# Rotary embedding on one core: 2 MB slabs in place of 1 MB tiles, small pieces at both ends, tables ordered anew

## The chip, the cores and the metric

The kernel runs on one core of one Trainium2 chip. The metric is the device time of one execution in microseconds, the median of ten runs. The engines that matter are VectorE (DVE in the profile), GpSimd (POOL), ScalarE (ACT), SyncE (SP), and the core's 16 DMA engines, which carry everything between HBM and the on-chip memory. SP and ScalarE each own a queue of transfers.

## The reference

`x` is float32 of shape (8, 2048, 8, 64): batch, position, head, channel. `cos` and `sin` are (2048, 32). The last axis of `x` is cut into halves and rotated by the position's angles:

```python
x1 = x[..., :32]; x2 = x[..., 32:]
cos = cos[None, :, None, :]; sin = sin[None, :, None, :]
out1 = x1 * cos - x2 * sin
out2 = x1 * sin + x2 * cos
return np.concatenate([out1, out2], axis=-1)
```

33.55 MB are read, 33.55 MB written, and the two tables are 256 KB each.

## The kernel before

The 2048 positions of a batch lie on the 128 partitions, 16 consecutive ones each (`R = 16`), so a partition's data of one batch are contiguous: 16 positions x 512 floats, 32 KB. A tile takes 4 positions (`SL = 4`) of one batch: 128 x 2048 floats, 1 MB, in rows of 8 KB. There are 32 tiles, and the loop takes all batches for the first four positions, then the next four. Twenty buffers (`xpool`) hold tiles.

The tables are loaded whole at the start by the ScalarE queue (lines 48 and 49), sin first; each is 128 x 512 floats in rows of 2 KB. VectorE makes from sin a table `ssin` with -sin and +sin for the two halves (lines 58 and 59) and copies cos into PSUM (`cos_ps`, line 60). The loads of all tiles stand in the sync queue (line 55).

A tile passes through three steps:
- POOL multiplies in two instructions of 128 x 1024 (line 73) the swapped halves of `xt` by `ssin` and writes `t2` in SBUF (three buffers).
- VectorE multiplies `xt` by cos (line 78) into `t1`, which lies in PSUM (one buffer).
- VectorE adds `t1` and `t2` into `xt` itself (line 83), and the ScalarE queue stores the tile (line 84).

The order of work is that of the program; the waits are set by a framework that follows which tile is read and written. A buffer of `xpool` is loaded again when the store from it has landed.

Of the kernel before, what the change touches and what calls it, by code (L numbers as in the profile page):

```python
# [2 lines left out]

# [4 lines left out]


@with_exitstack  # L10
def kernel(
    ctx: ExitStack,
    tc: tile.TileContext,
    x: bass.AP,
    cos: bass.AP,
    sin: bass.AP,
    out: bass.AP,
):
    nc = tc.nc
    f32 = mybir.dt.float32  # L20

    B, S, H, D = x.shape
    Dh = D // 2
    P = 128
    HD = H * D
    R = S // P

    SL = 4
    n_blk = R // SL
    FREE = SL * HD  # L30

    xv = x.rearrange("b (q r) h d -> b q (r h d)", q=P)
    ov = out.rearrange("b (q r) h d -> b q (r h d)", q=P)
    cos_src = cos.rearrange("(q r) d -> q r d", q=P)
    sin_src = sin.rearrange("(q r) d -> q r d", q=P)

    const_pool = ctx.enter_context(tc.tile_pool(name="const", bufs=1))
    cps_pool = ctx.enter_context(tc.tile_pool(name="cps", bufs=1, space=bass.MemoryType.PSUM))
    t1_pool = ctx.enter_context(tc.tile_pool(name="t1p", bufs=1, space=bass.MemoryType.PSUM))
    xpool = ctx.enter_context(tc.tile_pool(name="xpool", bufs=20))  # L40
    t2_pool = ctx.enter_context(tc.tile_pool(name="t2p", bufs=3))

    cos_sb = const_pool.tile([P, R, Dh], f32, tag="cb")
    sin_sb = const_pool.tile([P, R, Dh], f32, tag="sb")
    ssin = const_pool.tile([P, R, 2, Dh], f32, tag="ss")
    cos_ps = cps_pool.tile([P, R, Dh], f32, tag="cp")

    nc.scalar.dma_start(out=sin_sb, in_=sin_src)  # L48
    nc.scalar.dma_start(out=cos_sb, in_=cos_src)

    tiles = [(b, l) for l in range(n_blk) for b in range(B)]
    xts = []
    for i, (b, l) in enumerate(tiles):
        xt = xpool.tile([P, FREE], f32, tag="xt", name=f"xt{i}")
        nc.sync.dma_start(out=xt, in_=xv[b, :, l * FREE : (l + 1) * FREE])
        xts.append(xt)

    nc.vector.tensor_scalar_mul(ssin[:, :, 0, :], sin_sb, -1.0)  # L58
    nc.vector.tensor_copy(ssin[:, :, 1, :], sin_sb)  # L59
    nc.vector.tensor_copy(cos_ps, cos_sb)  # L60

    def rep(a, n):
        return dataclasses.replace(a, ap=[a.ap[0][:], a.ap[1][:], [0, n], a.ap[-1][:]])

    for i, (b, l) in enumerate(tiles):
        xt = xts[i]
        t1 = t1_pool.tile([P, FREE], f32, tag="t1")
        t2 = t2_pool.tile([P, FREE], f32, tag="t2")

        for u in range(2):  # L70
            dst = t2.rearrange("p (rh u d) -> p rh u d", u=2, d=Dh)[:, :, u, :]
            src = xt.rearrange("p (rh u d) -> p rh u d", u=2, d=Dh)[:, :, 1 - u, :]
            nc.gpsimd.tensor_mul(  # L73
                out=dst.rearrange("p (r h) d -> p r h d", h=H),
                in0=src.rearrange("p (r h) d -> p r h d", h=H),
                in1=rep(ssin[:, l * SL : (l + 1) * SL, u, :], H),
            )
        nc.vector.tensor_mul(  # L78
            out=t1.rearrange("p (r k d) -> p r k d", r=SL, d=Dh),
            in0=xt.rearrange("p (r k d) -> p r k d", r=SL, d=Dh),  # L80
            in1=rep(cos_ps[:, l * SL : (l + 1) * SL, :], 2 * H),
        )
        nc.vector.tensor_add(out=xt, in0=t1, in1=t2)  # L83
        nc.scalar.dma_start(out=ov[b, :, l * FREE : (l + 1) * FREE], in_=xt)


# [1 line left out]
_INS = ['x', 'cos', 'sin']  # L88
_OUTS = [((8, 2048, 8, 64), 'float32')]


# [23 lines left out]
```

## Time and profile before

| | us |
|---|---|
| median of 10 runs (168.19 to 168.55) | 168.3 |
| the profiled execution | 168.36 |
| its span on the core | 166.6 |
| VectorE busy, 67 instructions | 148.2 (89%) |
| GpSimd busy, 68 instructions | 146.3 (88%) |
| moved by DMA | 67.65 MB, mean 406 GB/s |

The span is what the profiler saw of the program on the core; the execution's own time is 1.76 us more. A busy figure counts instructions that compute, not those that issue transfers. The profile also has a chain of waits, which follows from the last instruction back to what released each step, groups of equal instructions with their mean duration and the idle time ahead of them, busy time and DMA rate for chosen stretches, and for each transfer the time from its issue to its landing.

### The profile page before, as it was taken

The numbers are of one execution on the slowest core, as the hardware profiler recorded it, in microseconds if no ns is written. First come the engines' busy times: TensorE is split into PE (matmuls) and PEld (weight loads), VectorE is DVE, ScalarE is ACT, GpSimd is POOL, SyncE is SP. The second block draws the span as 40 slices with busy tenths as digits, with TensorE's granted clock in tenths as the row PEclk, the third lists the DMA queues.
The fourth block names the chain that finished last, engine by engine and source line by source line (L and its number), as shares of the span: only waits on it lengthen the run. The fifth ranks groups of instructions, "written<-read, shape, count | busy, mean of one in ns | idle before, by whom it ended". The sixth has DMA issues, their size and how long they took to land.

```text
span 166.6 us, 381 instructions
## 1 busy us (share of the span) xinstructions
DVE 148.2 (89%) x67; POOL 146.3 (88%) x68
## 2 busy tenths in 40 slices
DVE  0169999999999999999999999999999999999980
POOL 0299999999999999999999999999999999998000
DMA  5999999999999999999999999999999999999656
GB/s 180 425 424 427 368 433 419 433 425 429 429 421 435 421 433 427 425 433 421 427 425 429 427 425 431 421 433 423 431 431 421 433 421 431 427 427 431 275 220 252
DMA packets 9506, 67.65 MB, mean 406 GB/s; under 512 B 1056, under 2 KB 1056, under 8 KB 1312
## 3 DMA queue, kind: packets, MB, share of 16 engines
q10 hardware_dynamic: 4896, 34.08, 48.6%
q1 hardware_dynamic: 4608, 33.56, 48.4%
q14 instruction: 2, 0.02, 0.0%
HBM read 34.08 MB, written 33.55 MB: 406 GB/s over the span
## 4 chain that ended last, share of the span: by engine, by line
DVE 89%; DMA 5%; issue 2%; DVEq 0%; ACTq 0%
DVE t L78 44%; DVE xt L83 44%; DMA cos_sb<-in_cos_dram 5%; DVE cos_ps L60 0%; DVEq L83 0%; ACTq L48 0%
## 5 line engine op out<-in xcount | busy, mean ns | idle before, releaser
L73 POOL TENSOR_TENSOR t<-xt,ssin 128x1024 f32<-128x1024 f32 x64 | 146.1, 2318 | 6.8 <-DVE ssin L58 6.8
L83 DVE TENSOR_TENSOR xt<-t,t 128x2048 f32<-128x2048 f32 x32 | 73.3, 2292 | 3.3
L78 DVE TENSOR_TENSOR t<-xt,cos_ps 128x2048 f32<-128x2048 f32 x32 | 73.5, 2295 | 1.1
L58 DVE TENSOR_SCALAR ssin<-sin_sb 128x512 f32<-128x512 f32 x1 | 0.4, 427 | 6.8 <-DMA sin_sb<-in_sin_dram 6.8
L60 DVE COPY cos_ps<-cos_sb 128x512 f32<-128x512 f32 x1 | 0.7, 695 | 2.4 <-DMA cos_sb<-in_cos_dram 2.4
L59 DVE COPY ssin<-sin_sb 128x512 f32<-128x512 f32 x1 | 0.4, 420 | 0.0
L99 POOL MEMSET const-float32-0.0<- 128x1 f32 x1 | 0.1, 98 | 0.2 <-issue 0.2
L99 POOL MEMSET const-bfloat16-1.0<- 128x1 bf16 x1 | 0.1, 101 | 0.0
L99 POOL MEMSET const-uint8-127<- 128x1 uint8 x1 | 0.1, 101 | 0.0
L99 POOL MEMSET const-float32-1.0<- 128x1 f32 x1 | 0.1, 98 | 0.0
## 6 DMA issues: line engine op xcount, KB each, us to landing
xt<-in_x_dram SPq DMA_DIRECT2D x32, 1024.0 KB, 20.8
out_dram<-xt ACTq DMA_DIRECT2D x32, 1024.0 KB, 11.3
sin_sb<-in_sin_dram ACTq DMA_DIRECT2D x1, 256.0 KB, 6.0
cos_sb<-in_cos_dram ACTq DMA_DIRECT2D x1, 256.0 KB, 8.7
```

Of the source, the lines that this page charges most:

```text
L58: nc.vector.tensor_scalar_mul(ssin[:, :, 0, :], sin_sb, -1.0)
L59: nc.vector.tensor_copy(ssin[:, :, 1, :], sin_sb)
L60: nc.vector.tensor_copy(cos_ps, cos_sb)
L73: nc.gpsimd.tensor_mul(out=dst.rearrange("p (r h) d -> p r h d", h=H), in0=src.rearrange("p (r h) d -> p r h d", h=H), in1=rep(ssin[:, l * ...
L78: nc.vector.tensor_mul(out=t1.rearrange("p (r k d) -> p r k d", r=SL, d=Dh), in0=xt.rearrange("p (r k d) -> p r k d", r=SL, d=Dh), in1=rep ...
L83: nc.vector.tensor_add(out=xt, in0=t1, in1=t2)
L99: nc = _bacc.Bacc("TRN2", target_bir_lowering=False, num_devices=1)
```

## The change

Transfers become 2 MB slabs of 8 positions (`SL = 8`, rows of 16 KB), in 10 buffers. VectorE and GpSimd still work on units of 4 positions, 128 x 2048 floats (`UNIT`), except in the first and the last slab. Slab 0 is loaded and worked on in pieces of 1, 1, 2 and 4 positions (512, 512, 1024 and 2048 floats a partition); the last slab is loaded whole, and worked on and stored in pieces of 4, 2, 1 and 1. All other slabs are stored whole, after their second unit.

The order of the tables is new: x's first piece of 256 KB leads the sync queue, then sin on the same queue, then the rest of x; cos leads the ScalarE queue. `ssin` is gone: GpSimd reads sin itself for the second half, which it now computes first, and a table `nsin` for the first half, made by ScalarE (`nc.scalar.mul`). The first ten slabs' loads are issued ahead of the loop; each later one stands behind the store of the slab whose buffer it takes.

```diff
-    SL = 4
-    n_blk = R // SL
-    FREE = SL * HD
+    SL = 8
+    n_half = R // SL
+    SLAB = SL * HD
+    UNIT = 4 * HD
+    NBUF = 10
...
-    ssin = const_pool.tile([P, R, 2, Dh], f32, tag="ss")
+    nsin = const_pool.tile([P, R, Dh], f32, tag="ns")
...
-    nc.scalar.dma_start(out=sin_sb, in_=sin_src)
+    def cuts(i):
+        if i == 0:
+            return [HD, HD, 2 * HD, UNIT]
+        return [SLAB]
+
+    def pieces(i):
+        if i == 0:
+            return [HD, HD, 2 * HD, UNIT]
+        if i == last:
+            return [UNIT, 2 * HD, HD, HD]
+        return [UNIT, UNIT]
+
+    def stores(i):
+        return pieces(i) if i == last else [SLAB]
...
+    def load(i):
+        b, l = slabs[i]
+        xt = xpool.tile([P, SLAB], f32, tag="xt", name=f"xt{i}")
+        for lo, n in spans(cuts(i)):
+            nc.sync.dma_start(
+                out=xt[:, lo : lo + n],
+                in_=xv[b, :, l * SLAB + lo : l * SLAB + lo + n],
+            )
+            if i == 0 and lo == 0:
+                nc.sync.dma_start(out=sin_sb, in_=sin_src)
+        xts[i] = xt
+
     nc.scalar.dma_start(out=cos_sb, in_=cos_src)
+    for i in range(NBUF):
+        load(i)
...
-    nc.vector.tensor_scalar_mul(ssin[:, :, 0, :], sin_sb, -1.0)
-    nc.vector.tensor_copy(ssin[:, :, 1, :], sin_sb)
+    nc.scalar.mul(nsin, sin_sb, -1.0)
     nc.vector.tensor_copy(cos_ps, cos_sb)
...
+        for u, tab in ((1, sin_sb), (0, nsin)):
             nc.gpsimd.tensor_mul(
+                out=t2u[:, :, u, :].rearrange("p (r h) d -> p r h d", h=H),
+                in0=xu[:, :, 1 - u, :].rearrange("p (r h) d -> p r h d", h=H),
+                in1=rep(tab[:, r0 : r0 + nr, :], H),
             )
...
+    for i, (b, l) in enumerate(slabs):
+        done = 0
+        st = list(spans(stores(i)))
+        for lo, n in spans(pieces(i)):
+            rotate(i, lo, n)
+            done = lo + n
+            while st and st[0][0] + st[0][1] <= done:
+                slo, sn = st.pop(0)
+                nc.scalar.dma_start(
+                    out=ov[b, :, l * SLAB + slo : l * SLAB + slo + sn],
+                    in_=xts[i][:, slo : slo + sn],
+                )
+        if i >= 1 and i - 1 + NBUF <= last:
+            load(i - 1 + NBUF)
```

`spans` yields start and length of each piece; `rotate` does the three steps on one piece.

More of the change, by code (lines that the diff above doesn't have):

```diff
@@ L20 @@
     f32 = mybir.dt.float32
+    PSUM = bass.MemoryType.PSUM
     B, S, H, D = x.shape
@@ L37 @@
     const_pool = ctx.enter_context(tc.tile_pool(name="const", bufs=1))
-    cps_pool = ctx.enter_context(tc.tile_pool(name="cps", bufs=1, space=bass.MemoryType.PSUM))
-    t1_pool = ctx.enter_context(tc.tile_pool(name="t1p", bufs=1, space=bass.MemoryType.PSUM))
-    xpool = ctx.enter_context(tc.tile_pool(name="xpool", bufs=20))
+    tab_pool = ctx.enter_context(tc.tile_pool(name="tab", bufs=1, space=PSUM))
+    t1_pool = ctx.enter_context(tc.tile_pool(name="t1p", bufs=1, space=PSUM))
+    xpool = ctx.enter_context(tc.tile_pool(name="xpool", bufs=NBUF))
     t2_pool = ctx.enter_context(tc.tile_pool(name="t2p", bufs=3))
@@ L44, with spans @@
     sin_sb = const_pool.tile([P, R, Dh], f32, tag="sb")
-    ssin = const_pool.tile([P, R, 2, Dh], f32, tag="ss")
-    cos_ps = cps_pool.tile([P, R, Dh], f32, tag="cp")
-    nc.scalar.dma_start(out=sin_sb, in_=sin_src)
-    nc.scalar.dma_start(out=cos_sb, in_=cos_src)
[L51 to L58, printed above, removed]
-    nc.vector.tensor_copy(ssin[:, :, 1, :], sin_sb)
+    nsin = const_pool.tile([P, R, Dh], f32, tag="ns")
+    cos_ps = tab_pool.tile([P, R, Dh], f32, tag="cp")
+    slabs = [(b, l) for l in range(n_half) for b in range(B)]
+    last = len(slabs) - 1
+    xts = {}
+    def cuts(i):
[10 more added lines that the diff above has]
+        return pieces(i) if i == last else [SLAB]
+    def spans(sizes):
+        lo = 0
+        for n in sizes:
+            yield lo, n
+            lo += n
+    def load(i):
[9 more added lines that the diff above has]
+        xts[i] = xt
+    nc.scalar.dma_start(out=cos_sb, in_=cos_src)
+    for i in range(NBUF):
+        load(i)
+    nc.scalar.mul(nsin, sin_sb, -1.0)
     nc.vector.tensor_copy(cos_ps, cos_sb)
@@ L63, in rep, with rotate @@
         return dataclasses.replace(a, ap=[a.ap[0][:], a.ap[1][:], [0, n], a.ap[-1][:]])
[L65 to L72, printed above, removed]
+    def rotate(i, lo, n):
+        b, l = slabs[i]
+        xt = xts[i][:, lo : lo + n]
+        r0 = l * SL + lo // HD
+        nr = n // HD
+        t1 = t1_pool.tile([P, n], f32, tag="t1")
+        t2 = t2_pool.tile([P, n], f32, tag="t2")
+        xu = xt.rearrange("p (g u d) -> p g u d", u=2, d=Dh)
+        t2u = t2.rearrange("p (g u d) -> p g u d", u=2, d=Dh)
+        for u, tab in ((1, sin_sb), (0, nsin)):
@@ L73 @@
             nc.gpsimd.tensor_mul(
-                out=dst.rearrange("p (r h) d -> p r h d", h=H),
-                in0=src.rearrange("p (r h) d -> p r h d", h=H),
-                in1=rep(ssin[:, l * SL : (l + 1) * SL, u, :], H),
+                out=t2u[:, :, u, :].rearrange("p (r h) d -> p r h d", h=H),
+                in0=xu[:, :, 1 - u, :].rearrange("p (r h) d -> p r h d", h=H),
+                in1=rep(tab[:, r0 : r0 + nr, :], H),
             )
         nc.vector.tensor_mul(
-            out=t1.rearrange("p (r k d) -> p r k d", r=SL, d=Dh),
@@ L80 @@
-            in0=xt.rearrange("p (r k d) -> p r k d", r=SL, d=Dh),
-            in1=rep(cos_ps[:, l * SL : (l + 1) * SL, :], 2 * H),
+            out=t1.rearrange("p (r k d) -> p r k d", r=nr, d=Dh),
+            in0=xt.rearrange("p (r k d) -> p r k d", r=nr, d=Dh),
+            in1=rep(cos_ps[:, r0 : r0 + nr, :], 2 * H),
         )
         nc.vector.tensor_add(out=xt, in0=t1, in1=t2)
-        nc.scalar.dma_start(out=ov[b, :, l * FREE : (l + 1) * FREE], in_=xt)
+    for i, (b, l) in enumerate(slabs):
[12 more added lines that the diff above has]
+            load(i - 1 + NBUF)
```

## The prediction

> **What bounds the kernel now.** I read the chain of waits first, because it ends where the kernel ends. In order of time (start, length, what), its pieces are:
>
> ```profile
> 1.16 8.74 DMA cos_sb<-in_cos_dram
> 9.93 0.71 DVE cos_ps L60
> 10.66 2.31 DVE t L78
> 13.06 2.30 DVE xt L83
> ...
> 157.14 2.31 DVE t L78
> 159.54 2.29 DVE xt L83
> ```
>
> After a 10.66 us wait for cos and its copy to PSUM, VectorE (DVE) runs 32 pairs of multiply and add until 161.84: 151.2 / 32 = 4.725 us a pair. Nothing interrupts it. The last 1 MB store is issued at 161.86; its line in the trace gives 3.9 us to landing, so 165.8, and the span closes 0.8 later at 166.6. DVE is the bound, together with its late start and the naked last store.
>
> Next, the groups of instructions (busy, mean ns | idle before, releaser):
>
> ```profile
> L73 POOL TENSOR_TENSOR t<-xt,ssin 128x1024 f32<-128x1024 f32 x64 | 146.1, 2318 | 6.8 <-DVE ssin L58 6.8
> L83 DVE TENSOR_TENSOR xt<-t,t 128x2048 f32<-128x2048 f32 x32 | 73.3, 2292 | 3.3
> L78 DVE TENSOR_TENSOR t<-xt,cos_ps 128x2048 f32<-128x2048 f32 x32 | 73.5, 2295 | 1.1
> L60 DVE COPY cos_ps<-cos_sb 128x512 f32<-128x512 f32 x1 | 0.7, 695 | 2.4 <-DMA cos_sb<-in_cos_dram 2.4
> ```
>
> GpSimd (POOL) needs 146.1 / 32 = 4.57 us a tile and starts 3.4 us before DVE, so it is never late. Last, busy time by stretch (DVE, POOL, clock, DMA share, GB/s):
>
> ```profile
> 1.00:2.00 1.00, 0.00 (x0) 0.00 (x0) 1.00 0.59 82
> 2.00:3.00 1.00, 0.00 (x0) 0.00 (x0) 1.00 0.56 180
> 15.00:20.00 5.00, 4.86 (x3) 5.00 (x3) 1.00 1.00 382
> 20.00:80.00 60.00, 58.20 (x27) 60.00 (x27) 1.00 1.01 427
> 80.00:150.00 70.00, 68.02 (x30) 70.00 (x32) 1.00 1.01 427
> 155.00:160.00 5.00, 4.86 (x3) 0.00 (x0) 1.00 0.73 305
> 160.00:166.60 6.60, 1.83 (x1) 0.00 (x0) 1.00 0.44 181
> ```
>
> The DMA engines are full at 427 GB/s from 3 to 150 us, and slack only at the end. That is a **second bound just below the first**: 0.26 MB have moved by 3.0, the other 67.39 of the page's 67.65 MB take 157.8 us at 427, the dip at 15 to 20 costs 5 x 45/427 = 0.5, so the last byte cannot move before 161.3. With 1.45 us of receipt (3.9 less 1.05 MB / 427 = 2.46) and the 0.8, the floor is a span of 163.6. Whatever compute gains beyond 3.0 us is lost there.
>
> **What the Trainium skill says.** "DMA: Bandwidth & Descriptors", section "Queues, rings and completion order": each DMA engine takes turns between queues packet by packet. The trace agrees: sin (2 KB rows) landed at 6.8, the first x tile (8 KB rows, four times the bytes) at 0.7 + 5.6 = 6.3. So against 8 KB rows a table gets one byte in five; against 2 KB rows, one in two. "SBUF — State Buffer", "Who interferes with whom": a DVE instruction with two SBUF inputs contends with GpSimd's reads. Here each has one PSUM input, before and after, and L83 keeps 2291 to 2292 ns beside a busy POOL.
>
> **The change part by part.**
>
> *Tables at the front.* cos (scalar queue) now shares only with x's first 2 KB rows: both are through after 0.52 MB. By the stretches 0.26 MB have moved at 3.0, so this is 3.6 us, plus receipt. Receipt here: x's first tile and sin together were 1.31 MB, moved by 5.5, landed 6.3 and 6.8, so 0.8 to 1.3. cos lands at 4.4 to 4.9. sin follows x's first piece on the sync queue: 0.79 MB, moved by 4.25, landed 5.1 to 5.6; I take 5.4. SP now issues six transfers before x's second slab, at 0.33 to 0.55 us each (the row of L55), every one ahead of the bytes.
>
> *-sin on ScalarE.* L58 and L59 (427 + 420 ns) leave DVE. The trace has no ScalarE arithmetic. The skill's "ScalarE: Activation LUTs", "What ACT_TABLE_LOAD costs", gives 186 ns + 0.833 per element: 0.61 us for 512, ready at 6.0. POOL uses raw sin first, and its first operation takes 0.65 us, so this is just hidden. A table load (1.3 us, with its drain 2.7, same section) depends on no data: ahead of the cos issue it delays cos to some 6.2 at 1.3 us, 7.6 at 2.7. DVE's own work on the first slab (0.7 and 10.4, below) would then end at 17.3 or 18.7, where POOL lets it end at 17.3, so the cost is 0 to 1.4 us; less than nothing it cannot give. I take 0. Stores sit behind -sin on ScalarE's queue, but the first comes 11 us later.
>
> *More pieces.* cos_ps at 695 ns for 512 elements and L78 at 2295 for 2048 give 1.042 ns an element and 162 ns fixed; with the gap in the period (4.725 - 4.587, halved: 69 ns) an additional DVE instruction costs 0.23 us. Four additional pieces, two in each end slab, are 8 instructions, 1.85 us. For POOL no small form is shown. "GPSIMD Engine Reference", section 3, has 4497 ns for 2048; with the trace's 2318 for 1024 that is 2.13 ns an element and 139 fixed (bounds 0 to 185): 0.65 us for 256 elements and 1.19 for 512, less the 35 ns by which its instructions overlap (2318 against 2283 pitch).
>
> *The start then goes by POOL.* From 5.4: pieces of 512 end at 6.7 and 8.0, 1024 at 10.4, 2048 at 15.0. DVE waits for each and adds the last by 17.3 (cos at 4.9 plus 0.7 plus 10.4 of its own would give 16.0). Then 30 units x 4.725 = 141.75 and two additional pieces, 0.92: DVE ends at **160.0**, against 161.84. The next units of POOL (19.6, 24.1) come just before DVE wants them (19.6, 24.4). So the 6 us earlier table is worth 1.9 at the end: POOL's lead is gone and the pieces are paid for.
>
> *Small last store.* 256 KB: 1.45 + 0.61 = 2.06 in place of 3.9. 160.0 + 0.05 + 2.06 + 0.8 = 162.9 by DVE.
>
> *2 MB transfers.* Same bytes, and the same buffer space (10 x 2 MB for 20 x 1 MB). A slab's store waits for the whole slab: the first goes out at about 17.4 (15.4 before), and until then loads have the engines alone. A whole slab must have landed before its first unit starts. Loads before landed every 4.9 us once stores ran (issue plus landing: 20.1, 25.0, 29.9, 34.9, 39.8). At 9.82 us a slab: x loads have 6.4 MB when contention begins at 18.7 (1.2 after issue, as before), the other 27.1 MB at half of 427 take 127, so the last slab lands near 147; POOL must have it by 147.3, 2.3 before DVE's turn at 149.6. Earlier slabs have more room (the eighth 3 us). It just fits, so I charge 0.
>
> *Sum.* Compute gives 162.9, the DMA floor 163.6 with nothing idle. The larger decides: 3.0 us below the profiled 166.6. The profiled execution took 168.36, 1.76 outside its span; the median of the runs is 168.3. So 163.6 + 1.76 - 0.06 = **165.3 us**.
>
> **Rivals.**
> 1. *Longer rows carry faster.* The floor rests on 427 GB/s with 8 KB rows; stretches of the page reach 435. At 1% more the floor is 162.1 and DVE decides: 162.9 + 1.7 = 164.6; with a 0.5 us faster POOL start, 164.1. For it: less overhead per row. Against: the engines' share already reads 1.01.
> 2. *The last slab is late (slower).* Loads and stores share at packet turns, and the fit above has 0.3 us. From a landing L, POOL needs 4.57 for the first unit, DVE then 7.7 for its add and the small pieces, and 2.9 follow: the span is L + 15.2. It decides from L = 148.4 and is slower than before from 151.4. If loads get 47% in place of half, 27.1 MB take 135, L = 154.9, span 170.1, time **171.8**. For it: no slack, and a slab asked for whole. Against: before, the last load was issued at 114.9 and landed 22.9 later, at 137.8, so loads had more than half; and every byte a load loses a store gains.
> 3. *Longer rows carry worse.* 1.9% off 427 lifts the floor by 3.0 us and eats the gain; 4% gives 168.6 + 3 = about 171.6. Nothing in this trace shows 16 KB rows.
> 4. *The early start does nothing,* because some load is not there in the first slabs: POOL late by another 3.7 us, 162.9 + 3.7 + 1.7 = 168.3. The second slab needs 4.72 MB moved, 13.4 + 1.2 = 14.6 against POOL's 15.0, so this too is close, but later slabs have 5 us.
>
> **How the numbers follow.** A measurement of this kernel tells about 0.2%, 0.3 us, from no change. Chances: the forecast (165.0 to 166.6, a wait of up to 1.3 us in it) 0.58; rival 1 0.24; rival 2 0.08; rival 3 0.05; rival 4 0.05, of which 0.03 within 0.2% and 0.02 just faster. Of rivals 2 and 3, 0.02 are mild and still faster. Faster 0.86, same 0.03, slower 0.11. The range reaches down through rival 1, to 163.9, and up past the forecast with a longer table load or a mild rival 2, to 167.2: about 0.83.
>
> **What would show it.** cos and sin landed before 6; POOL's first instruction near 5.4, then POOL the releaser of DVE's first three or four adds and no one after; DVE's last add near 160 (later if the last slab was); the DMA row full until 160 and ending steeply; additional DVE pieces of 0.70 and 1.23 us; the last store about 2 us. I am wrong if DVE shows waits for x late in the run (rival 2), if the middle stretches leave 427 by over 1% (1 or 3), or if DMA stands idle before the end although compute was early.

## The result and the profile after

The changed kernel takes **165.19 us** (median of 8 runs, 165.04 to 165.47) against 168.28 us for the kernel before beside it: ratio 0.9818, 95% interval 0.9809 to 0.9826. The forecast was 165.3 us. The profiled execution took 164.97, its span is 163.2.

The chain of waits of the changed kernel (start, length, what) answers to the one shown of before:

```profile
1.16 4.29 DMA sin_sb<-in_sin_dram
5.59 4.32 POOL t L108 x6
10.73 4.62 POOL t L108 x2
15.38 2.30 DVE xt L118
17.71 2.31 DVE t L113
...
145.24 2.31 DVE t L113
149.97 2.31 DVE t L113
```

The 10.66 us wait for cos is gone. The chain now begins with sin, passes through eight products on POOL and only then, at 15.38, comes to VectorE (DVE), which it doesn't leave again. The timeline of the start (start, length, engine, what, idle time and releaser) shows how they hand over:

```profile
1.16 1.28 ACT L92 ACT_TABLE_LOAD   x1 [1.16 <-PEq L148]
...
5.47 0.63 ACT L92 ACTIVATE nsin<-sin_sb 128x512 f32<-128x512 f32 x1 [3.03 <-DMA sin_sb<-in_sin_dram]
5.59 0.73 POOL L108 TENSOR_TENSOR t<-xt,sin_sb 128x256 f32<-128x256 f32 x1 [5.15 <-DMA sin_sb<-in_sin_dram]
...
6.28 0.72 POOL L108 TENSOR_TENSOR t<-xt,nsin 128x256 f32<-128x256 f32 x1
...
7.03 0.69 DVE L118 TENSOR_TENSOR xt<-t,t 128x512 f32<-128x512 f32 x1 [0.69 <-POOL t L108]
...
15.38 2.29 DVE L118 TENSOR_TENSOR xt<-t,t 128x2048 f32<-128x2048 f32 x1 [1.01 <-POOL t L108]
```

-sin is ready at 6.10, just ahead of the first product that reads it (6.28). DVE waits for POOL three times, 2.0 us in all, the last time for the 2048 piece; after that not once. Its last add is over at 160.30 (161.84 before):

```profile
158.81 0.70 DVE L113 TENSOR_TENSOR t<-xt,cos_ps 128x512 f32<-128x512 f32 x1
159.61 0.69 DVE L118 TENSOR_TENSOR xt<-t,t 128x512 f32<-128x512 f32 x1
```

The last store, 256 KB, is issued at 160.33 and lands 2.0 us later; the span ends 0.85 after that. The stretches (length, then busy time of DVE, ScalarE and POOL, clock, DMA share, GB/s):

```profile
0.00:22.00 22.00, 14.70 (x11) 1.91 (x2) 16.61 (x15) 1.00 0.93 363
22.00:150.00 128.00, 124.28 (x56) 0.00 (x0) 125.81 (x56) 1.00 1.01 431
150.00:155.00 5.00, 4.86 (x3) 0.00 (x0) 4.21 (x6) 1.00 0.99 423
155.00:160.00 5.00, 4.62 (x6) 0.00 (x0) 1.14 (x2) 1.00 0.95 390
160.00:163.00 3.00, 0.30 (x1) 0.00 (x0) 0.00 (x0) 1.00 0.39 148
```

The first stretch holds the start and a dip when the first stores set in (287 GB/s from 20 to 22 us). From 22 us on the DMA engines move 431 GB/s where the kernel before moved 427, and they are nearly full until 160. The trace's landings say it more sharply: the last stores land at 152.3, 157.15, 159.6, 160.9 and 161.5, each behind the one before by its own bytes at about 430 GB/s. Only the very last finds an empty queue. Had it been queued it would have landed at 161.5 + 0.6 = 162.1; it landed at 162.35. So **compute and transfers end within 0.3 us of each other**.

What the result leaves open is which of the three parts brought it: the front (order of tables, first pieces), the tail (last pieces) or the 2 MB transfers, to which the prediction gave nothing.

### The profile page after: what moved, and what is told of

Read it like the earlier page. It is cut to its first block, busy times and chain, and to the rows that moved or that the text cites. A ratio compares the mean times of both kernels' runs of the same rounds, so it can differ in the third digit from the quotient of the medians.

```text
span 163.2 us, 331 instructions
## 1 busy us (share of the span) xinstructions
DVE 148.8 (91%) x73; ACT 1.9 (1%) x2; POOL 147.8 (91%) x76
## 4 chain that ended last, share of the span: by engine, by line
DVE 87%; POOL 5%; DMA 3%; issue 2%; DVEq 0%; SPq 0%; POOLq 0%
DVE xt L118 44%; DVE t L113 43%; POOL t L108 5%; DMA sin_sb<-in_sin_dram 3%; DVEq L118 0%; SPq L80 0%; POOLq L108 0%
## 5 line engine op out<-in xcount | busy, mean ns | idle before, releaser
L108 POOL TENSOR_TENSOR t<-xt,sin_sb 128x1024 f32<-128x1024 f32 (+2 forms) x36 | 75.3, 2092 | 8.1 <-DMA sin_sb<-in_sin_dram 5.2
L118 DVE TENSOR_TENSOR xt<-t,t 128x2048 f32<-128x2048 f32 (+2 forms) x36 | 74.0, 2054 | 5.4 <-POOL t L108 2.0
L108 POOL TENSOR_TENSOR t<-xt,nsin 128x1024 f32<-128x1024 f32 (+2 forms) x36 | 75.4, 2095 | 0.0
L113 DVE TENSOR_TENSOR t<-xt,cos_ps 128x2048 f32<-128x2048 f32 (+2 forms) x36 | 74.1, 2059 | 1.2
L92 ACT ACTIVATE nsin<-sin_sb 128x512 f32<-128x512 f32 x1 | 0.6, 630 | 3.0 <-DMA sin_sb<-in_sin_dram 3.0
```

The lines of the kernel that those rows point to most:

```text
L92: nc.scalar.mul(nsin, sin_sb, -1.0)
L108: nc.gpsimd.tensor_mul(out=t2u[:, :, u, :].rearrange("p (r h) d -> p r h d", h=H), in0=xu[:, :, 1 - u, :].rearrange("p (r h) d -> p r h d" ...
L113: nc.vector.tensor_mul(out=t1.rearrange("p (r k d) -> p r k d", r=nr, d=Dh), in0=xt.rearrange("p (r k d) -> p r k d", r=nr, d=Dh), in1=rep ...
```

## The experiments

My theory: two bounds lie close together, VectorE's chain and the sum of the transfers, and each part moves one of them. Rivals: the size of the transfers does it alone; the floor of the transfers decides alone; a whole slab comes late. Each kernel is the changed one with the edit shown. Medians, and ratios to the kernel before in the same comparison (its median is 168.22 to 168.28 in all of them):

| kernel | us | ratio, 95% interval |
|---|---|---|
| the change | 165.19 | 0.9818 (0.9809 to 0.9826) |
| e1, 1 MB transfers | 166.77 | 0.9906 (0.9893 to 0.9920) |
| e2, tables change places | 165.04 | 0.9812 (0.9793 to 0.9832) |
| e3, tail undone | 166.29 | 0.9887 (0.9872 to 0.9902) |
| e4, front undone | 167.85 | 0.9979 (0.9972 to 0.9986) |
| e5, little arithmetic, 2 MB | 164.52 | 0.9772 (0.9751 to 0.9793) |
| e6, little arithmetic, 1 MB | 166.26 | 0.9879 (0.9862 to 0.9895) |
| e7, only stores 1 MB | 165.35 | 0.9825 (0.9810 to 0.9841) |
| e8, two pieces fewer | 165.11 | 0.9811 (0.9797 to 0.9826) |
| e9, size alone | 168.84 | 1.0037 (1.0024 to 1.0049) |
| e10, only loads 1 MB | 165.75 | 0.9852 (0.9831 to 0.9872) |
| e11, front of e8, tail kept | 165.00 | 0.9811 (0.9797 to 0.9824) |
| e12, -sin on VectorE | 165.50 | 0.9836 (0.9822 to 0.9849) |

**e1, 1 MB transfers both ways.**

```diff
     def cuts(i):
...
-        return [SLAB]
+        return [UNIT, UNIT]
...
     def stores(i):
-        return pieces(i) if i == last else [SLAB]
+        return pieces(i) if i == last else [UNIT, UNIT]
```

> The changed kernel with 1 MB transfers (rows of 8 KB) in place of 2 MB, loads and stores, in the same ten slab buffers; tables, first and last pieces as in the change. My theory: the size is worth nothing in itself, VectorE's chain sets the end as before: 165.2 us within 0.4, VectorE's last add near 160.3. Rival (longer rows carry faster): the middle stretches fall from about 430 back to 427 GB/s, the floor of the transfers rises by about 1.1 us and the time is 166 or more. Second rival (a whole slab of 2 MB is late for POOL): POOL's waits for x, 1.6 us in the change, vanish and the time falls by a few tenths.

The size is worth 1.6 us here, and my theory's "nothing" is refuted. VectorE's chain did not move, though: its last add is over at 160.45. The stretches of e1 show what did:

```profile
0.00:22.00 22.00, 14.59 (x11) 1.91 (x2) 16.49 (x15) 1.00 0.92 353
22.00:150.00 128.00, 124.27 (x55) 0.00 (x0) 128.00 (x58) 1.00 1.01 427
155.00:160.00 5.00, 4.62 (x6) 0.00 (x0) 1.28 (x2) 1.00 1.00 422
160.00:163.00 3.00, 0.45 (x1) 0.00 (x0) 0.00 (x0) 1.00 0.78 309
```

Against the change, 10 GB/s are missing for 22 us and 4 for 128: 0.22 + 0.51 = 0.73 MB, which take 1.7 us at 427 (each kernel's dip at its first stores lies in the first stretch). They are carried at the end: in 160 to 163 the engines are still 78% busy (39% in the change), and the last store lands 3.6 us after its issue in place of 2.0, queued behind the others. POOL's waits for x (1.6 us in the change) are indeed gone, as the second rival said, and that gained nothing.

**e3, the tail undone** (`[UNIT, 2 * HD, HD, HD]` becomes `[UNIT, UNIT]`).

> The changed kernel without the small last pieces: the last slab is worked on and stored in two units of 1 MB. My theory: VectorE ends 0.92 us earlier (four instructions of 0.23 fewer), 159.4, then 0.05 + 3.9 + 0.8: span 164.1, time about 166.1, that is the small pieces bring 0.9 us net. Rival (the end is set by the sum of the transfers): no difference, 165.2 to 165.4, because the DMA engines are full to 160 either way.

166.29 us, as the chain has it: VectorE ends at 159.61, its last 1 MB lands 3.8 us after the issue. Against the change VectorE gained 0.7 and the store lost 1.8.

**e4, the front undone.**

```diff
-            return [HD, HD, 2 * HD, UNIT]
+            return [UNIT, UNIT]
...
-            if i == 0 and lo == 0:
-                nc.sync.dma_start(out=sin_sb, in_=sin_src)
...
+    nc.scalar.dma_start(out=sin_sb, in_=sin_src)
     nc.scalar.dma_start(out=cos_sb, in_=cos_src)
```

The first two lines stand for `cuts` and `pieces` alike.

> The changed kernel without the new front: sin, then cos on the scalar queue, first slab loaded and worked on in two units of 1 MB; -sin still made by ScalarE, small last pieces kept. My theory: cos lands at 9.9 and VectorE starts at 10.6 as in the kernel before, ends at 10.6 + 151.2 + 0.92 = 162.8, span 165.7, time about 167.6: the front brings 2.4 us of the 3.1. Rival (the front's gain is lost at the floor of the transfers): 166 or less.

167.85 us. VectorE's copy of cos starts at 9.64 and its last add ends at 162.86, 2.56 later than in the change; 0.53 of that is one wait in mid run, which e9 comes back to. Here the transfers are clearly not the bound; they run dry before the end:

```profile
150.00:155.00 5.00, 4.77 (x4) 0.00 (x0) 1.96 (x3) 1.00 0.42 177
```

**e2, the tables change places** (`sin_sb` and `cos_sb` exchanged in the two issues).

> Only the two tables change places: sin leads the scalar queue, cos follows x's first piece on the sync queue. My theory: POOL's start sets VectorE's end, and POOL waits for sin, not cos. sin then lands near 4.9 in place of 5.4, POOL starts 0.5 us earlier, cos at 5.4 still comes in time (VectorE needs it by about 5.5), the last add moves from 160.3 to about 159.8 and the time to about 164.7. Rival (the floor of the transfers decides): the last add moves but the last landing doesn't, 165.2. Rival (cos sets the start): 165.5 or more.

Inconclusive: 165.04, with runs from 164.72 to 165.59; two of the four are at the 164.7 of my theory. In the profiled execution, one of the longer ones, POOL did start at 4.70 in place of 5.59, but then waited 1.22 us for x's third piece and VectorE's first slab ended at 18.17 in place of 17.70. In this trace the earlier table helped only until x's third piece was wanted, which landed at 8.61 in place of 7.40.

**e5 and e6, the transfers with little arithmetic.** In `rotate` the two products on POOL and the multiply are left out, and the add reads x and cos (the new line is shortened):

```diff
-        nc.vector.tensor_add(out=xt, in0=t1, in1=t2)
+        nc.vector.tensor_add(out=xt..., in0=xt..., in1=rep(cos_ps[:, r0 : r0 + nr, :], 2 * H))
```

e6 has e1's edit too.

> The changed kernel with most of the arithmetic left out: GpSimd's two products and VectorE's multiply are gone, VectorE does one add of x and cos a piece; all transfers as in the change. What is left is the floor of the transfers. My theory (with 2 MB transfers compute and floor end together): the floor is 161.5 + 0.6 for the last 256 KB, plus 0.85: span about 163.0, time 164.5 to 165.0, hardly less than 165.2 though VectorE's work is halved. Rival (compute alone sets the end of the changed kernel): the time falls to 163.5 or less.

> The same with 1 MB transfers both ways. My theory after e1: shorter rows move at 427 in place of 431 GB/s, so the floor is 1.5 to 2 us higher whatever the arithmetic: 166.4 to 166.8, as in e1. Rival (the 1.6 us of e1 came from waits between compute and transfers): 165.2 or less.

The page of e5 (busy us, share, instructions) and two of its stretches:

```profile
DVE 72.9 (45%) x37; ACT 1.9 (1%) x2; POOL 0.2 (0%) x4
...
20.00:80.00 60.00, 27.03 (x13) 0.00 (x0) 0.00 (x0) 1.00 1.01 432
80.00:150.00 70.00, 31.40 (x14) 0.00 (x0) 0.00 (x0) 1.00 1.01 431
```

With half of VectorE's work and all of POOL's gone the time falls from 165.19 to 164.52: 0.7 us are all that lies between the change and its transfers. With 1 MB transfers the same kernel takes 166.26, 1.7 us more, and the whole arithmetic of e1 adds only 0.5 to that. By the profiled spans, 163.0 (e5), 164.2 (e6) and 165.1 (e1), it is 1.2 and 0.9; e6 spends 2.2 us outside its span where the others spend 1.8, for a cause that isn't seen. By either count the larger part of the 1.6 us of e1 is there with hardly any arithmetic: the size acts on the floor of the transfers, not on waits between them and compute.

The two queues on the pages (packets, MB, share of 16 engines' span), first of e5, then of e6, show where it lies:

```profile
q1 hardware_dynamic: 2880, 33.82, 49.5%
q10 hardware_dynamic: 2880, 33.82, 48.7%
...
q1 hardware_dynamic: 5040, 33.82, 49.8%
q10 hardware_dynamic: 5040, 33.82, 48.9%
```

For the same bytes the engines worked 98.2% of 163.0 us in e5 and 98.7% of 164.2 in e6: 160.1 and 162.1. In the traces' record of single rows a row of 16 KB took 611 ns on its engine and one of 8 KB 309 (medians), so two short rows cost 7 ns more than a long one. For the 3840 long rows of e5, on 16 engines, that is 1.7 us (an estimate). The rows alone make up the difference; whether the smaller number of transfers adds anything to it isn't told apart.

**e9, the size alone** (edits of e3 and e4 together).

> The kernel before with 2 MB transfers and nothing else of note: tables as before, first and last slab in two units of 1 MB, the last stored as two of 1 MB (-sin stays on ScalarE). My theory: the size lowers only the floor of the transfers, which lies under VectorE's chain there. Chain 10.6 + 151.2, then 3.9 + 0.85: 168.2 to 168.4, no change, though the same step is worth 1.6 us once front and tail are in. Rival (the size is worth 1.6 us by itself): 166.7.

Not faster but slower, by 0.6 us: 168.84. The rival, 166.7, is far off. The profiled execution has VectorE's first multiply at 10.88 in place of 10.66 and one wait of 0.53 us, so that the last 1 MB goes out at 162.48 in place of 161.86:

```profile
89.31 2.29 DVE L117 TENSOR_TENSOR xt<-t,t 128x2048 f32<-128x2048 f32 x1 [0.53 <-POOL t L107]
```

POOL is named, but it had finished this tile's products at 84.69, 4.6 us before the add, so it wasn't late. The same half microsecond stands before the same instruction, the 17th add of VectorE, in the traces of e4 (88.80), e8 (81.59) and e11 (81.53), and in no other kernel with the full arithmetic. These four take the first slab in two or three pieces. What the add waits for isn't seen. 2 MB transfers alone don't bring it, for the change, e2, e3 and e12 have them without it. If every execution of e9 has it, e9 would be near 168.3 without it (an estimate), no change, as my theory had it.

**e7 and e10, one direction each** (the `stores` line of e1 alone, the `cuts` line of e1 alone).

> The changed kernel with stores of 1 MB, loads of 2 MB. Tells apart which direction the size matters in. If rows of both directions count alike: 166.0. If only loads' rows matter: 165.2. If only stores' rows (or their number) matter: 166.8, as e1.

> The changed kernel with loads of 1 MB (rows of 8 KB) beside stores of 2 MB (rows of 16 KB). My theory, from the turns packet by packet: the stores' queue now takes two bytes of three while both have work, loads land every 7.3 us per 1 MB in place of 4.9, POOL and VectorE wait for x from about 30 us on, and the last load lands late. The transfers stay full until then (34.1 MB of loads and what is computed of the stores, 30 MB, at 427: about 154), and from there compute and last stores take 12 to 15 us: 168 to 171, slower than the change by 3 us or more. Rival (queues share by bytes): 166.8, as with 1 MB both ways.

e7 lost 0.16 us, within its interval, e10 0.6, both together (e1) 1.6: neither direction alone accounts for it. The stretches from 80 to 150 stand in order, 431 for the change, 429 (e7), 428 (e10), 427 (e1). That would fit a floor a little under VectorE's chain, where the first part of a loss costs nothing; no run tests this further.

In e7 the turns can be seen: beside stores with rows of 8 KB the loads with rows of 16 KB land every 7.3 us (22.4, 29.7, 37.0, 44.3), 287 of 429 GB/s, two bytes of three. In e10 my theory foresaw the reverse, loads starved, 168 us or more, and that is refuted; the waits of e10 (who for whom: us, times, longest) have no wait for x at all:

```profile
POOL t L108 <- DVE xt L118: 3.2, 2, 2.4
...
DVE xt L118 <- POOL t L108: 2.0, 3, 1.0
```

The loads' landings show why. While a store is moving they come 7.3 us apart (59.5 to 66.8, 70.0 to 77.3), as the turns would have it, but between two stores 3.0 to 3.6 (46.1 to 49.7, 56.5 to 59.5, 66.8 to 70.0). VectorE makes stores no faster than 222 GB/s, 2.1 MB in 9.45 us; at two bytes of three each is through before the next comes, and the loads then have the engines to themselves (425 of 427 GB/s from 38 to 40 us). Turns decide only while both queues have work.

**e8 and e11, fewer pieces.** e8 has e2's edit, the first slab in `[2 * HD, 2 * HD, UNIT]` and the last in `[UNIT, 3 * HD, HD]`; e11 keeps the tail of the change.

> A candidate: sin leads the scalar queue and cos follows x's first piece; the first slab in pieces of 2, 2 and 4 positions, the last in 4, 3 and 1, that is two pieces fewer in all. My theory: POOL starts near 5.4 with a piece of 1024 and ends the first slab at 14.7 in place of 15.3, VectorE ends 0.6 earlier from the front and 0.46 from the tail, near 159.2; then the floor of the transfers decides, lowered by 0.3 for want of 2 KB rows of x: time about 164.5. Rival (the first slab's end is set by when x lands): 165.0 or more.

> A candidate: the changed kernel with sin at the head of the scalar queue, cos behind x's first piece, and the first slab in pieces of 2, 2 and 4 positions; tail as in the change. My theory: VectorE's chain is 0.35 us shorter (its first unit of the second slab starts at 17.35 in place of 17.7, as in e8), last add near 159.95, last landing 161.9 to 162.1: 164.8 to 165.0. Rival (the floor alone decides): 165.1 to 165.3.

165.11 and 165.00: no difference from the change that can be told. Each moved what it should and met the next bound. Both had VectorE's second slab earlier (17.36 and 17.28 for 17.71), and both lost it again to the half microsecond before the 17th add; its timeline line in e11:

```profile
81.53 2.29 DVE L118 TENSOR_TENSOR xt<-t,t 128x2048 f32<-128x2048 f32 x1 [0.53 <-DVE t L113]
```

Here the releaser named is VectorE itself, and POOL's products had been ready since 78.83. In e8 the piece of three positions came out so late (158.41) that the DMA engines fell to 330 GB/s in 155 to 160, and the last store queued behind it.

**e12, -sin on VectorE** (`nc.scalar.mul(nsin, sin_sb, -1.0)` becomes `nc.vector.tensor_scalar_mul`).

> -sin made by VectorE in place of ScalarE, ahead of the copy of cos; no table load, no ScalarE arithmetic. My theory: VectorE's first add moves from 7.0 to 7.3 but POOL sets the end of the first slab, so the last add and the time don't move: 165.2 within 0.3. Rival (VectorE's 0.43 us lies on the path): 165.6.

165.50, 0.3 above the change, the intervals overlapping: my 0 and the rival's 0.4 aren't told apart. The trace shows another mechanism than either. The instruction came after the first multiply, and POOL waited 0.36 us for its second table; sin itself landed 0.3 later than in the change. In this trace, the longest of the four, POOL's delay moved the end, not the 0.45 us that VectorE spent.

## Why the prediction was right, and where it was not

*Start by POOL:* right. POOL started at 5.59 (5.4 predicted), ended the first slab at 15.3 (15.0), VectorE followed at 17.7 (17.3) and ended at 160.3 (160.0). The 0.3 us are sin's landing, 0.05 later than assumed plus 0.1 from landing to the first product, and products of 0.68 and 1.22 us pitch where 0.65 and 1.19 were taken. The estimate for small forms, from the trace's 2318 ns and the Trainium skill's "GPSIMD Engine Reference", section 3, thus held to 5%.

*-sin on ScalarE:* right. The Trainium skill's "ScalarE: Activation LUTs", "What ACT_TABLE_LOAD costs", gives 613 ns for 512 elements, by an estimate from its 186 ns and 0.833 an element, and 1.28 us for the load; the trace has 630 and 1.28. The load came after the cos issue and delayed nothing.

*Small last store:* right, 2.02 us for 2.06. e3 puts the tail at 1.1 us with its cost in VectorE instructions paid (0.9 expected).

*The floor of the transfers, 163.6:* this term was mis-sized, twice in opposite ways. It took the start of the kernel before and the rate of 8 KB rows. The new front moves fewer bytes at first: over the first 22 us 363 GB/s in the change and 353 in e6, where the kernel before moved 368. With it and 8 KB rows the floor is e6's span, 164.2, 0.6 above the term. The 16 KB rows then brought it down to e5's span, 163.0, just under the change's own 163.2.

*2 MB transfers, "I charge 0":* right as to lateness, for no slab held VectorE up. But the sum also gave the size no gain, by keeping 427 GB/s for 16 KB rows, and this step failed: they moved 431, and with front and tail in the size is worth 1.6 us (e1), half the gain. So the closeness of the forecast is in part luck. The floor, which the sum let decide, had two errors that nearly cancelled, and VectorE's chain, put at 162.9, measured 163.2 and was no longer under it. Rival 1 had the mechanism (1% more rate, VectorE then decides, 164.6) and was given a chance of 0.24; with POOL's 0.3 us in it, it is close to what happened.

*The last slab is late (rival 2):* it was close, as said. The slabs landed every 9.72 us (9.82 predicted), the last at 145.4 (147), and POOL stood waiting for four of the last slabs, half a microsecond each. VectorE never noticed, for it needed POOL's first product pair of the last slab only at 152.4 and had it at 150.2. e10, which was meant to bring this rival out, did not.

*The parts don't add.* Undone one at a time, front, tail and size cost 2.7, 1.1 and 1.6 us, together 5.4 for a change worth 3.1; the size alone costs 0.6 (the half microsecond of e9 is in the 2.7 and in the 0.6). Front and tail shorten VectorE's chain until it meets the floor; the size lowers the floor, which is worth something only then.

*Slips without effect:* SP issues five transfers ahead of x's second slab, not six. The cos table comes some 5 us earlier, not 6, and by the prediction's own figures that is worth 1.8 at the end, not 1.9.

## What to carry to other kernels

Before a chain is shortened, add up the other full resource to its end, last landing included: here the sum of the transfers lay 3.0 us below the chain by the estimate, and 2.4 by e6, which has the new front. Price it with the rows that the new kernel will have, not the old ones: 4 GB/s over 128 us, 1.2 us, was as large as the tail. And when a part is tested alone and shows nothing, ask under which bound it lies before it is dropped.

## What the runs showed of the hardware

- Two queues with work got equal numbers of rows: loads with 16 KB rows beside stores with 8 KB rows had 287 of 429 GB/s (e7), and loads with 8 KB rows beside stores with 16 KB rows landed 1 MB in 7.3 us while a store was moving (e10).
- With transfers in both directions, rows of 16 KB moved 431 GB/s (the change, 22 to 150 us), rows of 8 KB 427 (e1), one of each 429 and 428 (e7 and e10, 80 to 150 us).
- A row took its engine 84 ns at 2 KB, 159 at 4 KB, 309 at 8 KB and 611 at 16 KB (medians of e5 and e6): about 7 ns besides its bytes, an estimate from the last two.
- At the start, pieces with rows of 2 and 4 KB moved 0.14 MB less from 3 to 6 us than rows of 8 KB beside 2 KB tables.
